# Further products that nothing reads: in both preparations, in the context's chain and in the attention's cores

## The chip, the cores and the metric

The kernel runs on one core of one Trainium2 chip. The metric is the time of one execution on the device in microseconds (us). Engines: PE is TensorE (PEld its loading of weights), DVE is VectorE, ACT is ScalarE, POOL is GpSimd, SP issues the DMAs. Each has its own queue and works it off in order; between queues the engines wait for each other by semaphores. TensorE's clock is granted at one of two levels, 1.2 or 2.4 GHz; the profile gives it as 0.50 or 1.00, or as a mean over a stretch.

## What is computed

One layer of a hybrid backbone over 256 latent tokens with a context of 256 tokens, width 1024, in float32. The parts that matter here:

```python
h_x = modulate(rms_norm(x, norm1_g[l]), m_x[0], m_x[1])
h_c = modulate(rms_norm(ctx, norm1_g[l]), m_c[0], m_c[1])
z_x = split_cols(h_x @ w_in[l]); z_c = split_cols(h_c @ w_in[l])
ya_c, ya_x = rwkv_mixer(z_c, z_x, ...)       # both directions; latent scans start from the context's state
yb_c, yb_x = na_mixer(z_c, z_x, ...)         # windowed attention with all context keys
x = x + m_x[2] * branch_merge(z_x[9], z_x[10], ya_x, yb_x, proj_a[l], proj_b[l], w_out[l])
h2_x = modulate(rms_norm(x, norm2_g[l]), m_x[3], m_x[4])
x = x + m_x[5] * moe(h2_x, router_w, router_bias, moe_w1[l], moe_w3[l], moe_w2[l])
```

The scan of the mixer is, for each of 8 heads and both directions (`...` stands for what is left out):

```python
def rwkv_scan(s0, r, decay, k, v, kk, a, reverse, emit):
    def step(s, inp):
        w_t, k_t, v_t, kk_t, a_t = inp[:5]
        s_kk = jnp.einsum('bhvk,bhk->bhv', s, kk_t)
        s = (s * w_t[:, :, None, :]
             - s_kk[..., None] * (kk_t * a_t)[:, :, None, :]
             + v_t[..., None] * k_t[:, :, None, :])
        ...
```

## The kernel before

The scan runs in chunks of 32 steps. A stream (first the context, s = 0, then the latents, s = 1) passes three parts, which the names below follow.

- The preparation, `rw_prep`, for two halves f of the heads and two directions d: `low_rank` (products of 64 rows with 256 columns, L675, and ACT's tanh, L680); `decays` (DVE L692 to L710, ACT L694 to L700, POOL L705 to L711); `products` (small products within a chunk, L727, masked by DVE L733 and copied by ACT L736; then POOL scales their left operand, L739); `turn` (transposes L749, copied out by ACT and DVE, L753). POOL and DVE share `decays`: DVE L710 needs what POOL L709 writes.
- The solve, `rw_solve`: 31 steps on DVE (L790, L792).
- The chain, `rw_chain`: 8 steps, one chunk of each direction in each, with the products x (L820), the inverse (L826), y (L838) and, for latents, z (L852).

The first preparation lies from about 80 to 133 us, the context's chain from 183 to 250, the second preparation from 264 to 348, the latent chain from 385 to 441. Behind it come the merge and, from 512 us, the experts, which stream their weights.

Beside this own work runs a filler, the generator `others`: values, projections and core of the attention for two halves g (`att_proj`, `att_core`), receptances, the modulation's rows, gates. `fill()` in the own work takes as many steps of it as the next number in the table `FILL` says; the table is the same before and after. While a filler's step is emitted, `other[0]` is true. The core (`att_core`) makes scores (L990, 64 rows by 512 columns), softmax parts on DVE and ACT (L999 to L1005), transposes (L967) and the output (L975). The dense filler products are 128x256 and 128x512 from `arena_p` and `arena_q`.

The order on each engine isn't that of the text. The framework's planner makes it when the program is built, from the dependencies, the order of the text and estimates of its own of how long each instruction takes; it is then fixed. So added instructions can change the order of others, on other engines too.

PSUM has eight banks here, four as `pa` (filler) and four as `pb` (own work); a product into a new tile waits until the bank's last reader is through.

`warm(p, site, n)` puts products into PE's queue that nothing reads: bf16, 128 rows by 128 columns of weights, n columns streamed (512 or 256), written into the tile p that the next real products overwrite. `WARM` gives their number at a site. Before, the sites are the steps 3 to 7 of the latent chain and the group norm behind it. A dependency without a semaphore keeps such a product behind the last product of the own work (L276).

Of the kernel before, what the change touches and what calls it, by code (L numbers as in the profile page):

```python
# [166 lines left out]
]  # L167
ORDER = [(("k0", 1), ("k1", 0))] * 3

WARM = {(w, 1, i): n for w, n in (("x", 4), ("y", 3), ("z", 2)) for i in range(3, 8)}  # L170
WARM.update({("gn", i): n for i, n in enumerate((4, 4, 10, 3, 5, 5))})
MIX = [7, 1]
DEEP = [3]

# [58 lines left out]
def hybrid_kernel(ctx: ExitStack, tc: tile.TileContext, a, out, dbg=None, stop=None):  # L233
# [20 lines left out]
    def pa(name="pa"):  # L254
        return ps.tile([128, 512], F32, tag="a", name=name, bufs=4)

    def pb(name="pb"):
        return ps.tile([128, 512], F32, tag="b", name=name, bufs=4)
# [10 lines left out]
    def warm(p, site, n=512):  # L269


        cb = lambda k, w: cst1[:, _COFF[k][1] - NEARLY:_COFF[k][1] - NEARLY + w // 2].bitcast(mybir.dt.bfloat16)
        before = own[0]
        for _ in range(WARM.get(site, 0)):
            i = T.matmul(p[:, 512 - n:], cb("ob", 128), cb("scanm", n), start=True, stop=True, skip_group_check=True)  # L275
            tc.add_manual_dep(i.ins, before.name, ORDERED, reason="not before")  # L276

    def split(dhi, dlo, src, eng):

# [291 lines left out]
    p, p2 = fout["lw"]  # L571
# [89 lines left out]
    def rw_prep(s, R):  # L661
# [6 lines left out]
        def low_rank(f):  # L668
            for i, (b, src, o) in enumerate(((wlb, lw, 0), (alb, la, 8))):
                p2 = [pb(), pb()]  # L670
                for q in range(2):
                    for d in range(2):
                        r_ = slice(64 * d, 64 * d + 64)
                        Q = 2 * f + q
                        mm(p2[d][:, q * 256:(q + 1) * 256], b[r_, Q * 128:(Q + 1) * 128], src[r_, t_])  # L675
# [37 lines left out]
        def products(f, d):  # L713
# [2 lines left out]

            w = 32 * nw
            pp = [pb(), pb()]
            for i in range(8):
                if i and i % 2 == 0:  # L720
                    fill()
# [20 lines left out]
        def turn(f, d):  # L742
            bk = tmps[d][3]
            for q in range(2):
                if q:
                    fill()
                p = pb()
                for i in range(4):
                    T.transpose(p[:, i * 128:(i + 1) * 128], bk[:, q * 8 + 2 * i:q * 8 + 2 * i + 2].rearrange("p c w t -> p (c w t)"), ident)  # L749
                pv = p.rearrange("p (i h k) -> p i h k", i=4, h=2)  # L750
# [202 lines left out]
    def att_core(g):  # L953
# [26 lines left out]
        for q in range(2):  # L980
# [4 lines left out]
                G.tensor_tensor(bi.ap, bi.ap, C["win"].unsqueeze(1).to_broadcast([128, 6, 64]), op=ALU.add)  # L985
            for b in range(2):
                pls = [pa(), pa()]
                for h in range(2):
                    r_ = slice(64 * h, 64 * h + 64)
                    mm(pls[h], qB[r_, q, b * 128:(b + 1) * 128], kB[r_, q, :])  # L990
# [517 lines left out]
```

## Time and profile before

| | |
|---|---|
| median of 3 runs | 744.21 us (742.38 to 745.29) |
| the profiled execution | 747.27 us, of which the span is 745.5 us |
| mean granted clock of TensorE in the span | 0.957 |
| PE busy | 689.3 us, 92% of the span |
| DVE, ACT, POOL busy | 397.8, 299.5, 102.0 us |
| products that nothing reads | 82, all from 408 us on |

The rows come from the one profiled execution; times in them count from the start of its span. A row of a timeline merges instructions that follow each other on an engine: start, time, engine, line, operation, out<-in with shapes, number, and in brackets the idle time before it with what ended it. A float32 product of small shape stands in the trace as two records, so x64 there can be 32 products of the program. A row of the stretches gives the length, then for each engine its busy time and the number of its instructions, the granted clock, and the share and rate of the DMAs.

### The profile page before, as it was taken

What the parts mean: (1) busy time and instruction counts of PE and PEld (TensorE: products, weight loads), DVE (VectorE), ACT (ScalarE), POOL (GpSimd) and SP (SyncE); (2) the same over time, 40 slices, a digit from 0 to 9 for tenths busy, and PEclk for the clock granted to TensorE, in tenths of its full rate; (3) what the DMA queues carried; (4) which work ended last, traced back from release to release, by engine and by line L of the source; (5) the groups of instructions that cost most, each with busy time, mean ns of one, the idle gap of its engine ahead of it and who ended that gap; (6) DMA issues with size and microseconds to landing.
All of it is one profiled execution on the core that took longest, in us unless ns stands there. A gap on an engine that the chain in (4) does not pass through costs nothing.

```text
span 745.5 us, 14598 instructions
## 1 busy us (share of the span) xinstructions
PE 689.3 (92%) x6059; PEld 459.8 (62%) x6059; DVE 397.8 (53%) x738; ACT 299.5 (40%) x604; POOL 102.0 (14%) x90
## 2 busy tenths in 40 slices
PE   4998798999999977889899998998999999999996
PEld 2666677886775744467898775995435535534532
DVE  2546975997846478777985555954213113113113
ACT  5436667446655446836444432533201101101110
POOL 0001444002322024351003211000000000000000
PEclk9999969999995996889999999999999999999999
DMA  9843011231311132668671139888999999999951
GB/s 366 338 161 113 4 56 37 81 111 30 108 30 51 63 135 87 214 234 311 202 225 61 52 137 332 316 317 320 412 408 412 410 409 412 406 411 413 408 218 60
DMA packets 46297, 165.34 MB, mean 222 GB/s; under 512 B 5392, under 2 KB 6800, under 8 KB 45328
## 3 DMA queue, kind: packets, MB, share of 16 engines
q1 hardware_dynamic: 46224, 164.34, 58.9%
q8 instruction: 49, 0.80, 0.4%
q14 instruction: 24, 0.20, 0.1%
HBM read 163.27 MB, written 1.05 MB: 220 GB/s over the span
## 4 chain that ended last, share of the span: by engine, by line
PE 70%; DVE 11%; ACT 9%; issue 6%; POOL 3%; DMA 1%; DVEq 0%; SPq 0%; ACTq 0%; POOLq 0%
PE pa L264 51%; PE pb L264 15%; ACT arena L753 2%; DVE arena_q L281 2%; ACT arena L736 2%; PE pb L275 1%; ACT arena_q L280 1%; POOL arena L709 1%; DVE arena L790 1%; POOL arena L707 1%; DVE arena L792 1%; DMA arena<-in_x_dram 1%; DVE arena L710 1%; POOL arena L705 1%; DVE arena L693 1%
## 5 line engine op out<-in xcount | busy, mean ns | idle before, releaser
L264 PE MATMUL pa<-arena_p,arena_q 128*128 128x256 f32 (+1 forms) x984 | 163.6, 315 | 7.8 <-DVE arena_q L281 2.6
L264 PEld LDWEIGHTS pa<-arena_p,arena_q 128*128 128x128 f32 x984 | 134.8, 190 | 29.6 <-issue 7.0
L264 PE MATMUL pa<-arena,arena_m 128*64 128x512 f32 (+1 forms) x652 | 148.8, 561 | 0.0
L264 PE MATMUL pb<-arena 128*32 128x64 f32 (+13 forms) x2248 | 115.6, 279 | 22.0 <-DVE arena L710 7.3
L264 PEld LDWEIGHTS pb<-arena 128*32 128x32 f32 (+7 forms) x2246 | 72.9, 144 | 60.0 <-issue 24.0
L264 PEld LDWEIGHTS pa<-arena,arena_m 128*64 128x64 f32 x652 | 48.8, 138 | 85.1 <-issue 80.3
L280 ACT CAST arena_q<-arena 128x1024 fp32r<-128x1024 f32 (+1 forms) x66 | 63.0, 955 | 79.7 <-PE pa L264 57.7
L281 DVE TENSOR_TENSOR arena_q<-arena,arena_q 128x1024 fp32r<-128x1024 f32 (+1 forms) x66 | 77.5, 1174 | 24.0 <-ACT arena_q L280 18.8
L264 PE MATMUL pa<-arena_q,arena_p 128*128 128x256 f32 x384 | 57.5, 300 | 0.0
L1408 DVE TENSOR_TENSOR arena_m<-arena_m,pa 128x512 f32<-128x512 f32 x8 | 5.5, 688 | 95.9 <-PE pa L264 95.9
L264 PEld LDWEIGHTS pa<-arena_q,arena_p 128*128 128x128 f32 x384 | 50.2, 198 | 5.8 <-issue 3.2
L813 POOL TENSOR_TENSOR arena<-arena 64x512 f32<-64x512 f32 x30 | 33.9, 1130 | 127.9 <-DVE arena L843 126.1
L1349 ACT ACTIVATE arena_m<-pa,arena 128x128 f32<-128x128 f32 x32 | 12.0, 455 | 76.4 <-PE pa L264 76.4
L264 PE MATMUL pa<-arena_p,arena_m 128*64 128x512 f32 x140 | 41.3, 593 | 0.0
L264 PE MATMUL pa<-arena 128*64 128x256 f32 (+5 forms) x192 | 41.1, 470 | 0.0
L280 ACT CAST arena_r<-arena_m 128x512 fp32r<-128x512 f32 x16 | 9.9, 618 | 66.6 <-DVE arena_m L1428 66.6
L1428 DVE SCALAR_TENSOR_TENSOR arena_m<-pa,arena,arena_p 128x512 f32<-128x512 f32 x16 | 12.0, 751 | 44.8 <-PE pa L264 44.8
L809 ACT COPY arena<-arena 32x256 f32<-32x256 f32 x64 | 25.8, 403 | 20.5 <-PE pb L264 18.5
L264 PEld LDWEIGHTS pa<-arena_m,arena 128*128 128x128 f32 x256 | 29.2, 192 | 6.6 <-issue 5.7
L264 PE MATMUL pa<-arena_m,arena 128*128 128x128 f32 x256 | 30.7, 279 | 0.9 <-DVE arena_m L1336 0.9
L843 DVE TENSOR_TENSOR arena<-pb,arena 64x512 f32<-64x512 f32 x30 | 20.6, 688 | 15.5 <-PE pb L264 14.9
L264 PE MATMUL pb<-arena,arena 64*64 64x64 f32 (+1 forms) x496 | 28.0, 257 | 0.5 <-ACT arena L829 0.5
(210 smaller groups left out, 845.5 us busy)
## 6 DMA issues: line engine op xcount, KB each, us to landing
arena<-in_w_dram SPq DMA_DIRECT2D x137, 512.0 KB, 10.0
arena<-in_win_dram SPq DMA_DIRECT2D x42, 512.0 KB, 3.8
arena_p<-in_w_dram SPq DMA_DIRECT2D x35, 512.0 KB, 10.2
arena<-in_modr_dram SPq DMA_DIRECT2D x32, 512.0 KB, 4.1
arena<-in_modw_dram SPq DMA_DIRECT2D x4, 2048.0 KB, 14.5
arena<-in_w_dram SPq DMA_DIRECT2D x20, 256.0 KB, 8.2
arena_m<-in_w_dram SPq DMA_DIRECT2D x10, 512.0 KB, 8.8
arena<-in_pab_dram SPq DMA_DIRECT2D x8, 512.0 KB, 3.3
```

The costliest lines, as they stand in the source:

```text
L264: i = T.matmul(out, lhsT, rhs, start=start, stop=stop, skip_group_check=True)
L275: i = T.matmul(p[:, 512 - n:], cb("ob", 128), cb("scanm", n), start=True, stop=True, skip_group_check=True)
L280: S.copy(dhi.bitcast(F32R), src)
L281: eng.tensor_tensor(dlo.bitcast(F32R), src, dhi, op=ALU.subtract)
L693: V.tensor_tensor_scan(cum[:, go], C["scanm"], sg[:, go], 0.0, op0=ALU.mult, op1=ALU.add)
L736: S.activation(NT[ro + 32 * d:ro + 32 * d + 32, :, 2 * f:2 * f + 2].rearrange("p t q c -> p (q c) t")[:, par::2], pv[o_ + 32 * d:o_ + 32 * ...
L753: (V.tensor_copy if h and c2 else S.copy)(BT[f][64 - 64 * h:128 - 64 * h, d, q, c2:8:2, :], pv[64 * c2:64 * c2 + 64, :, h, :])
L809: S.copy(Z[rv, h, :, d, :], vt[32 * c4:32 * c4 + 32, h, tt, :, :])
L813: G.tensor_tensor(sd[r_], Z[r_, h], pc[r_, :, :, i].rearrange("p d q -> p q d").unsqueeze(3) .to_broadcast([64, 4, 2, 64]), op=ALU.mult)
L843: V.tensor_tensor(Z1[r_, h], pyv[r_], sd[r_], op=ALU.add)
L1349: S.activation(dst, src, AF.Identity, scale=m4[:, kc:kc + 1], bias=m3[:, kc:kc + 1])
L1428: V.scalar_tensor_tensor(sil.ap, py[n2], gsl[pr % 2].ap, m5r[:, n2 * 512:(n2 + 1) * 512], op0=ALU.mult, op1=ALU.mult)
```

## The change

`WARM` gets sites in both preparations (low-rank, products, turn), in steps 3 to 6 of the context's chain (x and y) and in the attention's core (before each pair of scores), and `warm` is called there. Within a filler's step the dependency on the own work's last product is left out. No other line changes.

```diff
--- before.py
+++ after.py
@@ -167,8 +167,16 @@
 ]
 ORDER = [(("k0", 1), ("k1", 0))] * 3
 
+
 WARM = {(w, 1, i): n for w, n in (("x", 4), ("y", 3), ("z", 2)) for i in range(3, 8)}
 WARM.update({("gn", i): n for i, n in enumerate((4, 4, 10, 3, 5, 5))})
+for _s in range(2):
+    for _f in range(2):
+        WARM.update({("low", _s, _f, i): 2 for i in range(2)})
+        WARM.update({("prod", _s, _f, d): 5 for d in range(2)})
+        WARM.update({("turn", _s, _f, d): 1 + _s for d in range(2)})
+    WARM["att", _s] = 4
+    WARM.update({(w, 0, i): n for w, n in (("x", 3), ("y", 2)) for i in range(3, 7)})
 MIX = [7, 1]
 DEEP = [3]
 
@@ -273,7 +281,8 @@
         before = own[0]
         for _ in range(WARM.get(site, 0)):
             i = T.matmul(p[:, 512 - n:], cb("ob", 128), cb("scanm", n), start=True, stop=True, skip_group_check=True)
-            tc.add_manual_dep(i.ins, before.name, ORDERED, reason="not before")
+            if not other[0]:
+                tc.add_manual_dep(i.ins, before.name, ORDERED, reason="not before")
 
     def split(dhi, dlo, src, eng):
 
@@ -668,6 +677,7 @@
         def low_rank(f):
             for i, (b, src, o) in enumerate(((wlb, lw, 0), (alb, la, 8))):
                 p2 = [pb(), pb()]
+                warm(p2[i], ("low", s, f, i))
                 for q in range(2):
                     for d in range(2):
                         r_ = slice(64 * d, 64 * d + 64)
@@ -716,6 +726,7 @@
 
             w = 32 * nw
             pp = [pb(), pb()]
+            warm(pp[0], ("prod", s, f, d), 256)
             for i in range(8):
                 if i and i % 2 == 0:
                     fill()
@@ -745,6 +756,7 @@
                 if q:
                     fill()
                 p = pb()
+                warm(p, ("turn", s, f, d))
                 for i in range(4):
                     T.transpose(p[:, i * 128:(i + 1) * 128], bk[:, q * 8 + 2 * i:q * 8 + 2 * i + 2].rearrange("p c w t -> p (c w t)"), ident)
                 pv = p.rearrange("p (i h k) -> p i h k", i=4, h=2)
@@ -985,6 +997,7 @@
                 G.tensor_tensor(bi.ap, bi.ap, C["win"].unsqueeze(1).to_broadcast([128, 6, 64]), op=ALU.add)
             for b in range(2):
                 pls = [pa(), pa()]
+                warm(pls[0], ("att", g))
                 for h in range(2):
                     r_ = slice(64 * h, 64 * h + 64)
                     mm(pls[h], qB[r_, q, b * 128:(b + 1) * 128], kB[r_, q, :])
```

That makes, with 512 columns: 16 in the low-rank, 24 before turns (1 per tile for the context, 2 for the latents), 8 in the chain's y, 32 in the cores; with 256 columns: 40 before `products`, 12 in the chain's x. The line numbers of after are higher, by 8 at `mm` (L264 is L272), 9 to 12 in the preparation (L709 is L719, L711 L721, L739 L750, L705 L715, L707 L717), 12 in the chain (L813 is L825) and 12 or 13 in the core (L967 is L979), and L275 is L283.

PE's queue at the first preparation, before, from the low-rank's tail (L264 into `pb`, 128x256) to the small products (64x32) of the first half and direction; `pa` from `arena_q` is filler:

```order
L264 MATMUL pb<-arena 128x256 x8
L264 MATMUL pa<-arena_q,arena_p 128x256 x23
L264 MATMUL pb<-arena 128x512 x4
L264 MATMUL pa<-arena_q,arena_p 128x256 x34
L264 MATMUL pb<-arena 64x32 x32
```

The same place after, first up to the first of five added products:

```order
L272 MATMUL pb<-arena 128x256 x4
L272 MATMUL pa<-arena_q,arena_p 128x256 x16
L272 MATMUL pb<-arena 128x512 x4
L283 LDWEIGHTS arena
L283 MATMUL pb<-arena 128x256
```

and from the fifth of them on:

```order
L283 MATMUL pb<-arena 128x256
L272 MATMUL pa<-arena_q,arena_p 128x256 x28
L272 MATMUL pb<-arena 64x32 x32
L283 LDWEIGHTS arena
L283 MATMUL pb<-arena 128x512
```

16 and 28 filler products stand ahead of the small products where 23 and 34 stood; the rest moved behind them. Two pairs of added products of 512 columns stand ahead of the first row shown.

PE's queue at the end of the first core, before, with the products of the context's chain (64x64 y, 32x64 x and inverse) between those of the attention (128x2, 128x512):

```order
L264 MATMUL pa<-arena_q,arena_p 128x256 x6
L264 MATMUL pb<-arena,arena_73 64x64 x8
L264 MATMUL pa<-arena 128x2 x3
L264 MATMUL pb<-arena,arena_73 64x64 x7
L264 MATMUL pa<-arena 128x2
L264 MATMUL pa<-arena 128x512
L264 MATMUL pb<-arena 32x64 x16
L264 MATMUL pa<-arena 128x512
```

And after, from the last products of that chain (64x64) on:

```order
L272 MATMUL pb<-arena,arena_73 64x64 x15
L272 MATMUL pa<-arena 128x512 x2
L272 MATMUL pa<-arena_q,arena_p 128x256 x6
L979 MATMUL pa<-arena 128x128 x4
L272 MATMUL pa<-arena_q,arena_p 128x256 x2
L272 MATMUL pa<-arena 128x2 x4
L272 MATMUL pa<-arena 128x512 x2
L979 MATMUL pa<-arena 128x128 x4
L283 LDWEIGHTS arena
L283 MATMUL pa<-arena 128x512
```

The chain is through before the 128x2 products, which lie two chain steps further back in it before.

POOL's queue in the second preparation, before (L709 `decays`, L739 behind `products`, L813 the latent chain's first step, L705 and L707 the second half's `decays`):

```order
L711 COPY arena<-arena 128x2x8
L739 TENSOR_TENSOR arena<-arena 128x1024
L709 TENSOR_TENSOR arena<-arena 128x512
L782 MEMSET arena 128x1024
L783 MEMSET arena 128x32
L711 COPY arena<-arena 128x16
L739 TENSOR_TENSOR arena<-arena 128x1024
L709 TENSOR_TENSOR arena<-arena 128x512
L711 COPY arena<-arena 128x2x8
L813 TENSOR_TENSOR arena<-arena 64x512 x2
L705 TENSOR_TENSOR arena<-arena 64x16x32
```

And after:

```order
L721 COPY arena<-arena 128x2x8
L719 TENSOR_TENSOR arena<-arena 128x512
L750 TENSOR_TENSOR arena<-arena 128x1024
L721 COPY arena<-arena 128x16
L794 MEMSET arena 128x1024
L795 MEMSET arena 128x32
L719 TENSOR_TENSOR arena<-arena 128x512
L750 TENSOR_TENSOR arena<-arena 128x1024
L721 COPY arena<-arena 128x2x8
L825 TENSOR_TENSOR arena<-arena 64x512 x2
L719 TENSOR_TENSOR arena<-arena 128x512
L715 TENSOR_TENSOR arena<-arena 64x16x32
```

L709 (now L719) stands ahead of L739 (L750) both times, and the fourth of its kind ahead of the second half's four L705 and L707 (L715, L717), behind which it stood.

## Rows read from the trace of the kernel before

**Rows 1.** The page's head, PE's busy time, and of the part with 40 slices PE's busy tenths and its granted clock in tenths.

```profile
span 745.5 us, 14598 instructions
PE 689.3 (92%) x6059; PEld 459.8 (62%) x6059; DVE 397.8 (53%) x738; ACT 299.5 (40%) x604; POOL 102.0 (14%) x90
...
PE   4998798999999977889899998998999999999996
...
PEclk9999969999995996889999999999999999999999
```

**Rows 2.** Stretches from the first preparation to the end of the second, cut where the clock changes; the columns are named in the first row.

```profile
core 0: us, PE busy (x) PEld busy (x) DVE busy (x) ACT busy (x) POOL busy (x), PEclk, DMA share, GB/s
90.60:107.50 16.90, 16.75 (x167) 13.10 (x171) 13.31 (x16) 10.16 (x23) 8.25 (x5) 0.50 0.20 63
107.60:132.80 25.20, 21.40 (x277) 17.97 (x271) 16.43 (x28) 20.35 (x45) 10.75 (x8) 1.00 0.14 43
183.00:222.00 39.00, 38.98 (x547) 29.90 (x547) 26.59 (x41) 22.13 (x47) 11.35 (x10) 1.00 0.22 66
227.10:244.00 16.90, 16.90 (x161) 8.78 (x164) 9.59 (x21) 7.90 (x18) 5.81 (x6) 0.50 0.09 29
244.20:263.70 19.50, 19.50 (x198) 16.42 (x191) 6.97 (x12) 8.56 (x19) 0.00 (x0) 1.00 0.24 82
263.70:278.20 14.50, 10.94 (x66) 4.69 (x64) 11.82 (x21) 8.84 (x22) 5.11 (x4) 1.00 0.33 114
278.30:281.60 3.30, 3.21 (x73) 2.19 (x73) 3.30 (x5) 1.73 (x4) 0.96 (x1) 0.50 0.37 133
281.70:288.40 6.70, 5.28 (x36) 2.75 (x36) 5.55 (x7) 2.79 (x7) 6.21 (x5) 1.00 0.58 192
288.60:302.00 13.40, 9.57 (x104) 6.61 (x108) 11.65 (x24) 10.68 (x25) 3.25 (x4) 0.50 0.22 72
302.20:325.90 23.70, 19.59 (x200) 11.31 (x192) 16.31 (x29) 16.50 (x36) 12.77 (x9) 1.00 0.63 211
326.10:332.80 6.70, 6.20 (x52) 4.83 (x53) 4.66 (x6) 2.29 (x4) 1.93 (x1) 0.50 0.68 242
332.90:348.50 15.60, 15.41 (x167) 12.74 (x167) 10.81 (x17) 11.40 (x24) 1.94 (x1) 1.00 0.81 289
```

**Rows 3.** Timeline of PE in the first preparation: filler, the wait for `decays`, and the filler with which the stretch of low clock ends.

```profile
76.44 2.96 PE L264 MATMUL pa<-arena_q,arena_p 128*128 128x256 f32 x23
...
81.80 4.25 PE L264 MATMUL pa<-arena_q,arena_p 128*128 128x256 f32 x34
90.58 3.94 PE L264 MATMUL pb<-arena 64*64 64x32 f32 x72 [4.53 <-DVE arena L710]
...
104.34 2.93 PE L264 MATMUL pa<-arena_q,arena_p 128*128 128x256 f32 x12
```

**Rows 4.** Timeline of PE in the context's chain, around 225 us.

```profile
223.73 0.68 PE L264 MATMUL pb<-arena,arena 64*64 64x64 f32 x16 [0.47 <-ACT arena L829]
224.34 0.83 PE L264 MATMUL pa<-arena 128*128 128x2 f32 x6
225.10 0.68 PE L264 MATMUL pb<-arena,arena 64*64 64x64 f32 x14
225.71 1.44 PE L264 MATMUL pa<-arena 128*128 128x2 f32 x4
227.07 1.34 PE L264 MATMUL pb<-arena 128*32 128x64 f32 x32
```

**Rows 5.** Timeline of PE in the latent chain: products that nothing reads (L275) and the product behind them.

```profile
411.71 0.82 PE L275 MATMUL pb<-arena 128*128 128x512 bf16 x3
412.46 0.33 PE L264 MATMUL pb<-arena,arena 64*64 64x64 f32 x2
...
416.20 0.61 PE L275 MATMUL pb<-arena 128*128 128x256 bf16 x4
416.74 0.30 PE L264 MATMUL pb<-arena 128*32 128x64 f32 x4
```

**Rows 6.** Timeline of PE in the second preparation: three rows with a wait before them.

```profile
278.39 4.31 PE L264 MATMUL pb<-arena 64*64 64x64 f32 x76 [1.61 <-DVE arena L710]
...
292.43 7.42 PE L264 MATMUL pb<-arena 64*128 64x256 f32 x92 [4.80 <-ACT arena L680]
...
326.60 1.22 PE L264 MATMUL pa<-arena_p,arena_q 128*128 128x256 f32 x4 [2.13 <-DVE arena_q L281]
```

**Rows 7.** Timelines of POOL (first four rows) and of DVE in the second preparation.

```profile
284.19 2.38 POOL L739 TENSOR_TENSOR arena<-arena 128x1024 f32<-128x1024 f32 x1
286.53 1.44 POOL L709 TENSOR_TENSOR arena<-arena 128x512 f32<-128x512 f32 x1
...
322.22 1.65 POOL L707 TENSOR_TENSOR arena<-arena 64x512 f32<-64x512 f32 x1
323.95 1.27 POOL L709 TENSOR_TENSOR arena<-arena 128x512 f32<-128x512 f32 x1
...
288.01 0.69 DVE L710 TENSOR_TENSOR arena<-arena 128x512 f32<-128x512 f32 x1 [1.15 <-POOL arena L709]
...
325.25 0.69 DVE L710 TENSOR_TENSOR arena<-arena 128x512 f32<-128x512 f32 x1 [2.43 <-POOL arena L709]
325.86 0.69 DVE L281 TENSOR_TENSOR arena_q<-arena,arena_q 128x512 fp32r<-128x512 f32 x1
```

## The prediction

> **What bounds the kernel now.** I read the slices first. TensorE (PE) is busy 92% of the span, and in the line of its granted clock the 6th, the 13th and the 16th to 18th slices are below 9 [rows 1]. Then I cut that part into stretches by the clock [rows 2]. There are five at 0.50, which is 1.2 GHz, and the others run at 1.00, 2.4 GHz. In the first two PE is busy all the time (16.75 of 16.90 us, and 16.90 of 16.90), so work there took twice as long on the engine that bounds it: 8.4 and 8.45 us could come back. The other three lie in the second preparation and hold 3.21, 9.57 and 6.20 us of PE work, so 1.6, 4.8 and 3.1 us at most. All five hold 26.3 us. Until 263.7 us PE hardly rests but before 90.58 us and at the first preparation's end, so up to there the work on PE sets the time. In the second preparation PE is idle for 13.7 of 83.9 us (the sum over the last seven stretches of [rows 2]), and there a chain through POOL, DVE and ACT sets it. What comes after 348.5 us is moved as a whole.
>
> The timelines show how the clock fell. Before 90.58 us PE waits 4.53 us for DVE [rows 3]; then it works at half speed on small products. At 224 us it is not idle, but does only 128x2 and 64x64 products for some 3 us, and the clock is at half from 227 on [rows 4].
>
> **What a product costs.** The kernel has them already in the latent chain: three of 512 columns take from 411.71 to the next product at 412.46, 0.75 us or 0.25 each; four of 256 take from 416.20 to 416.74, 0.135 each [rows 5]. The change adds 80 of 512 (16 low-rank, 24 before turns, 32 in the attention's cores, 8 in the chain) and 52 of 256 (40 and 12): 20.0 + 7.0 = 27.0 us, if all lies on the path. That is as much as the clock can give back, so the result hangs on what is hidden and on what comes back. By stage:
>
> First preparation, 16 of 512 and 20 of 256: 4.0 + 2.7 = 6.7 us. Nine of them (the second low-rank's four, the five that follow) run where the clock is low and cost double, 1.7 more: 8.4. The ten of 256 and eight of 512 behind 107.6 us (1.35 + 2.0 = 3.35) find PE idle for 3.8 of 25.2 us there, with ACT busy for 20.35 [rows 2]; I count them as covered by ACT's copies. Without this cover they cost the 3.35. Does the clock still fall? The order now has 16 + 28 filler products before the wait where it had 23 + 34. At 0.125 us (4.25 us for 34, [rows 3]) the 13 fewer save 1.6 us, and the nine products there cost 4 x 0.25 + 5 x 0.135 = 1.7. So PE arrives at the wait when it did, the wait of 4.53 us stays, and the clock falls. What changes is the way back. Before, the clock rose only behind twelve filler products in a row (104.34, [rows 3]); now full-width products stand between the small ones from the low-rank on, and I take half of the stretch as returned, 4.2 of 8.4 (bounds 0 and 8.4; a half because the fall itself is the same). Sum: 8.4 - 3.35 - 4.2 = +0.85.
>
> Context chain with the first core, 24 of 512 and 12 of 256: 6.0 + 1.6 = 7.6 us, nothing hidden, as PE is busy for 38.98 of 39.00, 16.90 of 16.90 and 19.50 of 19.50 us [rows 2]. The piece in which the clock fell, the 128x2 products with 64x64 around them, now stands behind the chain, between fillers, transposes and wide products, with four added ones before and four after. It is still thin there for some 4 us, so I expect a shorter fall, not none: two thirds back, 5.6 of 8.45 (bounds 0 and 8.45). Sum: +2.0.
>
> The Trainium skill (Trainium Kernel Development and Optimization, section "Performance Expectations") says that matmul busy time is a bad measure, since matmuls are pipelined, and that the busy share of weight loads is better. In the chain that share is 29.90 of 39.00 [rows 2], so by this rule about a quarter of the 7.6 would find room: the sum here would be +0.2 and the whole 1.8 us better. The products of [rows 5] stand between just such chain products and take their whole time, with a little more, so I keep the full price.
>
> Second preparation, 40 of 512 and 20 of 256: 10.0 + 2.7 = 12.7 us. The 12 and 5 before the first wait (3.7) fall into 3.65 us of idle PE up to 281.6 [rows 2], as PE waits for DVE L710 then [rows 6]: hidden. Eight and five belong to the second low-rank, the core and the product step behind it (2.7); about 1.5 goes into the wait of 4.80 us before 292.43, but two and five (1.2) come behind the release, on the path. Twelve before turns and in the core (3.0) lie beside ACT's copies, 4.11 us idle in the stretch up to 325.9: hidden. The last ten of 256 and eight of 512 (3.35) stand where PE is full (15.41 of 15.60): on the path. Together 4.55; if no cover held, 12.7.
>
> Here the new order gives something too. POOL has L739 before L709 [rows 7]: 2.38 us on which DVE L710 waits, and behind L710 in DVE's queue the reduce, ACT's copies and the release of PE at 292.43. Now L709 goes first: -2.4. The same happens at 325.25, where L710 waits 2.43 us for an L709 behind POOL's four L705 and L707, the filler's L281 is queued behind it, and PE idles for 2.13 us [rows 6, 7]. The new order has L709 ahead of these four, so -2.1. Bounds: nothing, if ACT's queue then waits for DVE's reduces anyway, and 4.5. I take 4.5, as these waits are rows and not guesses. L739 comes later for it; the turn waits on that, but behind ACT's copies. Of the clock: the first stretch's wait is filled, but the products before 278 us may not do (0.8 of 1.6); the wait before 292.43 only shrinks (1.6 of 4.8); the third went with the idle time now gone (2.1 of 3.1). Sum: 4.55 - 4.5 - 4.5 = -4.45.
>
> All: 0.85 + 2.0 - 4.45 = -1.6 us. The profiled execution took 747.27 us, so 745.7 for one like it; the median of the runs is 744.21, 3.1 lower, and so I predict 742.6 there. The unknown terms reach far: everything on the path and no clock back would be +28.7, everything hidden and all back -30.8. Neither end is near a row: in the chain products do cost, and in the second preparation PE does idle.
>
> **The rivals.**
> A, slower: in the stage where PE never rests the products are only more work, and clock falls as long as before, because it falls in waits and thin pieces that no product fills. Place: 73 to 263.7 us. Price: the 9.8 us that I took as returned. -1.6 + 9.8 = +8.2, 752.4 us. It decides once less than 4.5 of the 16.85 us comes back (then over 3.7 slower). For it: the wait of 4.53 us stays. Against: in the latent chain, with products in every step, the clock needs no filler to stay up.
> B, faster: from the context chain on the clock holds. Then 8.45 instead of 5.6, and 9.5 instead of 4.5: -1.6 - 2.85 - 5.0 = -9.45, 734.8 us. For it: the stretches at 1.00 hold many thin pieces. Against: waits of 4.80 and 1.61 us in the second preparation that depend on other engines.
> C: the order gives nothing. ACT L736 and PE wait for another queue and the 4.5 us of order stay: +2.9, 747.1 us. For it: the attention's reduces now stand together before the product step on DVE.
>
> **How the numbers follow.** Forecast 0.34 (own range 739.5 to 746), A 0.22, B 0.26, C 0.18. A measurement tells about 0.5%, 3.7 us, from no change. Faster by more: B and a fifth of the forecast, 0.33. Slower by more: A and a quarter of C, 0.26. Between: 0.41. The range, 736 to 750, leaves out the far halves of A and B.
>
> **What would show it.** Right: the clock still falls near 90 us but rises before 107; PE at 1.00 through the chain but for a short stretch in the thin piece behind it; DVE's waits for POOL L709 (1.15 and 2.43 us in [rows 7]) nearly gone; the last turn of the second preparation some 4 us earlier against the end of the context chain's dense filler. Wrong: a low stretch as long as before in the chain (A), none after 183 us (B), PE released for the second low-rank no sooner (C), or products that take clearly less than 0.25 us between chain products.

## The result and the profile after

The changed kernel takes 751.54 us (median of 5 runs, 751.17 to 756.94) against 742.38 us (5 runs, 741.9 to 745.29): a ratio of 1.0105, 95% interval 1.007 to 1.0139. The forecast was 742.6 us, its range 736 to 750. Timed once more beside the experiments, it is 1.0088 (1.0056 to 1.0121), +6.5 us. So it is slower: by 9.2 us between the first medians, by 7.8 and 6.5 us by the two ratios. One run of the kernel before, which took 2892.54 us, is left out everywhere.

There are two profiles of it, one of an execution of 756.94 us (span 755.1) and one (run a1_whole below) of 746.34 us (span 744.5). The kernel is the same and so is the order on each engine. Of the 10.6 us between the two, 3.2 lie ahead of the first preparation, and 7.4 behind, most of them where the clock falls in the one and not in the other. The second is the fastest of its ten runs (their median is 750.41 us), and the profile of before, 747.27 us, lies above its median. So from the first row below to the end the first is 9.2 us longer than before and the second only 1.8, and neither is the median's +6.5 by itself.

The page's slices of the first of them, which answer to [rows 1]:

```profile
PE   4998789999999887989999998998999999999996
PEclk9999899999999897999999999999999999999999
```

The clock line has three slices below 9, where it had five. The stretches of before, then of the two profiles of after. They are cut at: the semaphore that lets ACT through to the first tanh of the first preparation (L680, after L690), the first step of the first solve, the last ACT copy of the receptances (L924, after L936), the last DVE copy of a turn (L753, after L765) and, for the fourth row, DVE's last instruction of the group norm (L1184, after L1197). The end piece, 282.9 us before and 283.0 in both profiles of after, is left out. Columns as in [rows 2].

```profile
75.70:132.50 56.80, 48.13 (x507) 39.15 (x503) 43.65 (x58) 40.46 (x86) 24.45 (x18) 0.85 0.13 38
132.50:263.90 131.40, 130.06 (x1373) 98.50 (x1374) 91.60 (x177) 67.93 (x136) 23.75 (x22) 0.94 0.22 68
263.90:348.10 84.20, 70.00 (x688) 44.72 (x687) 64.57 (x102) 54.07 (x119) 32.27 (x24) 0.86 0.54 184
348.10:462.60 114.50, 107.64 (x1534) 88.09 (x1532) 76.94 (x149) 44.86 (x87) 15.79 (x16) 1.00 0.52 176
```

```profile
76.10:133.00 56.90, 47.22 (x535) 37.95 (x535) 42.54 (x58) 40.14 (x85) 24.37 (x18) 0.94 0.13 38
133.00:269.00 136.00, 131.62 (x1405) 99.74 (x1414) 91.51 (x177) 68.75 (x137) 25.57 (x22) 0.96 0.21 65
269.00:356.70 87.70, 75.19 (x721) 44.49 (x724) 63.73 (x101) 54.59 (x118) 31.20 (x24) 0.94 0.51 172
356.70:472.10 115.40, 110.19 (x1551) 90.76 (x1555) 76.73 (x150) 44.87 (x88) 16.84 (x16) 0.99 0.53 180
```

```profile
72.90:129.80 56.90, 46.75 (x535) 37.53 (x537) 42.51 (x57) 40.20 (x85) 24.39 (x18) 0.94 0.13 38
129.80:261.30 131.50, 128.01 (x1405) 97.96 (x1414) 90.81 (x177) 68.64 (x136) 25.02 (x22) 1.00 0.22 68
261.30:347.60 86.30, 74.75 (x722) 44.11 (x725) 63.13 (x101) 55.02 (x118) 31.23 (x24) 0.96 0.53 175
```

Read the second number (the length) and the clock against each other. In the first preparation the clock goes from 0.85 to 0.94, and the length stays at 56.8 to 56.9 us. (The tanh itself starts 2.0 us behind this cut before and 1.4 to 1.5 after, at 77.67, 77.53 and 74.38 us; measured from there the stage is 0.6 us longer in both profiles.) In the second it goes from 0.86 to 0.94 and 0.96, and the stage is longer by 3.5 and 2.1 us. There PE is busy for 5.2 and 4.75 us more, and its idle time (length less busy time), 14.2 us before, is 12.5 and 11.55 us: it is still there. In the context's stretch the two profiles differ by 4.5 us: one holds 1.00 and is as long as before, with 7.6 us of products in it, the other falls (0.96).

The first preparation in the PE timeline of the first profile, answering to [rows 3]:

```profile
82.44 3.61 PE L272 MATMUL pa<-arena_q,arena_p 128*128 128x256 f32 x28
90.35 1.93 PE L272 MATMUL pb<-arena 64*64 64x32 f32 x64 [4.30 <-DVE arena L720]
```

The wait of 4.53 us is still 4.30. The waits of PE in the second preparation, answering to [rows 6]:

```profile
283.38 2.10 PE L272 MATMUL pb<-arena 64*64 64x64 f32 x48 [3.30 <-DVE arena L720]
...
296.92 2.07 PE L272 MATMUL pb<-arena 64*128 64x256 f32 x4 [3.58 <-ACT arena L690]
...
337.30 1.01 PE L272 MATMUL pb<-arena 128*32 128x256 f32 x18 [2.13 <-DMA arena<-in_modr_dram]
```

The wait for the decays (L720) is 3.30 us where it was 1.61. The one before the second low-rank is 3.58 us where it was 4.80. At 337.30 it is a product of the modulation's rows, which waits for its DMA. That wait was there before, too, 2.09 us, just ahead of the first row of [rows 6]:

```profile
276.15 0.64 PE L264 MATMUL pb<-arena 128*32 128x256 f32 x8 [2.09 <-DMA arena<-in_modr_dram]
```

What stands behind the 4.80 us of before, in the chain of waits (start, us, what), from the decays of the stage's first direction to the release of PE:

```profile
277.56 0.69 DVE arena L710
...
288.01 0.69 DVE arena L710
288.70 0.61 DVE arena L1002
289.33 0.81 ACT arena L1003 x2
290.17 0.60 ACT arena L736
...
292.43 7.42 PE pb L264 x92
```

And behind the 3.58 us after:

```profile
282.63 0.69 DVE arena L720
...
289.17 1.68 DVE arena L718
290.84 0.60 DVE arena L720
291.44 0.41 DVE arena L1012
...
293.10 1.52 ACT arena L1016 x4
...
294.64 0.60 ACT arena L747
...
296.92 2.07 PE pb L272 x4
```

POOL is no longer in it: L720 follows L718 at once, where L710 waited 1.15 us for L709 [rows 7]. From the end of the first decays' L710 to the end of the second's it took 10.45 us before, and it takes 8.1 now. But the attention's softmax behind it (L1002 and L1003 before, L1012 to L1016 after) stands ahead of the copies and tanh (L747, L690) that release PE with 3.2 us where it had 1.5. The last piece, 2.3 us, is as before. So 2.3 us are gained, 1.7 lost again, and the whole way, 14.2 us before, is 13.6; in the second profile it is 13.6 too.

### The profile page after: what moved, and what is told of

Its sections match the earlier page's. It is cut to its first block, busy times and chain, and to the rows that moved or that the text cites. A ratio compares the mean times of both kernels' runs of the same rounds, so it can differ in the third digit from the quotient of the medians.

```text
span 755.1 us, 14826 instructions
## 1 busy us (share of the span) xinstructions
PE 697.7 (92%) x6170; PEld 461.9 (61%) x6191; DVE 395.4 (52%) x738; ACT 301.1 (40%) x604; POOL 103.8 (14%) x90
## 4 chain that ended last, share of the span: by engine, by line
PE 49%; DVE 7%; ACT 3%; DMA 2%; issue 1%; POOL 0%; DVEq 0%; ACTq 0%
PE pa L272 36%; PE pb L272 9%; PE pb L283 2%; DVE arena_q L290 2%; DMA arena<-in_win_dram 1%; DMA arena<-in_modr_dram 1%; ACT arena L747 1%; DVE arena L802 1%; PE pa L1426 0%; DVE arena L804 0%; ACT arena_q L289 0%; PE pa L1374 0%; DVE arena L720 0%; DVE arena L715 0%; DVE arena L703 0%
## 5 line engine op out<-in xcount | busy, mean ns | idle before, releaser
L272 PE MATMUL pa<-arena_p,arena_q 128*128 128x256 f32 (+1 forms) x984 | 162.5, 313 | 4.8 <-DVE arena_p L384 1.8
L272 PEld LDWEIGHTS pa<-arena_p,arena_q 128*128 128x128 f32 x984 | 133.7, 188 | 25.1 <-issue 5.2
L272 PE MATMUL pa<-arena,arena_m 128*64 128x512 f32 (+1 forms) x652 | 148.8, 561 | 0.0
L272 PE MATMUL pb<-arena 128*32 128x64 f32 (+13 forms) x2248 | 110.6, 265 | 20.2 <-DVE arena L720 7.6
L272 PEld LDWEIGHTS pb<-arena 128*32 128x32 f32 (+7 forms) x2246 | 68.6, 134 | 57.0 <-issue 16.6
L272 PEld LDWEIGHTS pa<-arena,arena_m 128*64 128x64 f32 x652 | 48.8, 138 | 85.1 <-issue 80.3
L290 DVE TENSOR_TENSOR arena_q<-arena,arena_q 128x1024 fp32r<-128x1024 f32 (+1 forms) x66 | 75.9, 1151 | 28.5 <-ACT arena_q L289 23.5
L272 PE MATMUL pa<-arena_q,arena_p 128*128 128x256 f32 x384 | 56.1, 293 | 0.0
L272 PEld LDWEIGHTS pa<-arena_q,arena_p 128*128 128x128 f32 x384 | 48.4, 190 | 4.5 <-issue 1.7
L825 POOL TENSOR_TENSOR arena<-arena 64x512 f32<-64x512 f32 x30 | 34.8, 1160 | 114.0 <-DVE arena L855 112.1
L283 PE MATMUL pb<-arena 128*128 128x256 bf16 (+1 forms) x165 | 37.0, 324 | 7.7 <-ACT arena L747 4.8
L272 PE MATMUL pa<-arena_p,arena_m 128*64 128x512 f32 x140 | 41.3, 593 | 0.0
L272 PE MATMUL pa<-arena 128*64 128x256 f32 (+5 forms) x192 | 35.3, 459 | 0.0
L272 PEld LDWEIGHTS pa<-arena_m,arena 128*128 128x128 f32 x256 | 29.2, 192 | 6.6 <-issue 5.7
L272 PE MATMUL pa<-arena_m,arena 128*128 128x128 f32 x256 | 30.7, 278 | 0.9 <-DVE arena_m L1349 0.9
L283 PEld LDWEIGHTS <-arena 128*128 128x128 bf16 x214 | 17.6, 100 | 20.5 <-issue 14.6
## 6 DMA issues: line engine op xcount, KB each, us to landing
arena_p<-in_w_dram SPq DMA_DIRECT2D x35, 512.0 KB, 10.2
```

What stands on the lines that cost most here:

```text
L272: i = T.matmul(out, lhsT, rhs, start=start, stop=stop, skip_group_check=True)
L290: eng.tensor_tensor(dlo.bitcast(F32R), src, dhi, op=ALU.subtract)
L825: G.tensor_tensor(sd[r_], Z[r_, h], pc[r_, :, :, i].rearrange("p d q -> p q d").unsqueeze(3) .to_broadcast([64, 4, 2, 64]), op=ALU.mult)
```

## The experiments

Two theories to begin with. Theory 1, added work: each part costs its products' time where PE has no rest, less the clock that it brings back in its own stage. Theory 2, new order: the loss is what the planner's new order does on the queues. Line numbers of the runs are those of after, or 2 to 6 higher. Where a ratio is turned into us, it is by the median of before that was timed beside the run (744.3 to 745.1 us). The times and ratios are of 6 to 12 runs; a stage's length is of the one profiled execution.

**The four parts alone.** Each keeps one part of the table's additions and leaves out the others. The first preparation:

```diff
+WARM.update({("low", 0, f, i): 2 for f in range(2) for i in range(2)})
+WARM.update({("prod", 0, f, d): 5 for f in range(2) for d in range(2)})
+WARM.update({("turn", 0, f, d): 1 for f in range(2) for d in range(2)})
```

> Only the first preparation's sites (16 products of 512 columns, 20 of 256, 6.7 us of TensorE time); the other four parts of the table as before. Theory 1 (added work): what the change costs is the products' time where TensorE has no rest, less the clock that they bring back in their own stage; then this part shows the +0.5 us that the stage up to the first solve showed in the whole change, and nothing behind it: 0 to +1 us in the total. Theory 2 (new order): the loss is the planner's new order behind the sites (attention behind the context's chain, waits moved in the second preparation, filler of the gates late); then this part alone, whose order differs from before far into the second preparation, already costs 3 to 5 us, and the time stands behind 133 us.

Measured: 1.0038 (1.0011 to 1.0066), +2.8 us, more than theory 1 and just less than theory 2 had. The profiled execution, 744.67 us, is one of its shorter ones. In it the first preparation takes 57.0 us, as before. In the two rows behind it no product was added, but the planner's order is another one. The second preparation takes 87.4 us instead of 84.2, with 15.9 us of idle time, which speaks for theory 2. The context's stretch takes 124.6 us instead of 131.4, for the clock holds at 1.00 in it:

```profile
131.10:255.70 124.60, 123.63 (x1372) 95.41 (x1376) 92.41 (x177) 68.84 (x137) 23.04 (x22) 1.00 0.22 67
255.70:343.10 87.40, 71.52 (x690) 44.19 (x687) 62.29 (x99) 54.51 (x119) 30.37 (x24) 0.88 0.56 187
```

The context's chain:

```diff
+WARM.update({(w, 0, i): n for w, n in (("x", 3), ("y", 2)) for i in range(3, 7)})
```

> Only the context chain's sites (8 products of 512 columns, 12 of 256, 3.6 us). The planner's order changes little here: POOL and SP stand as before, and only the chain's tail is arranged anew. Theory 1: +3.6 us less the part of the 8.45 us of the low stretch at 227 us that comes back, about +1 (0 to +2). Theory 2: as little order changes, about the same with the opposite cause: within +-1 us of before. This run prices the products with hardly any change of order, so it bounds theory 1: over +3 would mean that no clock comes back here.

Measured: 0.9959 (0.9939 to 0.9979), -3.1 us: faster than both kernels, and below what either theory expected. The stage, to be laid beside the second row of before above:

```profile
131.90:257.40 125.50, 123.94 (x1389) 96.72 (x1394) 91.03 (x177) 68.42 (x137) 23.75 (x22) 1.00 0.23 71
```

It is 5.9 us shorter, with 3.6 us of products more in it, and the clock holds at 1.00 throughout. If the products cost their full price, 9.5 us came back, for the 8.45 of [rows 2]. But the chain's tail also stands in another order here, and in p1_firstprep an order alone, without a product in this stretch, held the clock as well and made it 6.8 us shorter. So the gain is the change of table and order together; what of it is the products' no run separates.

The attention's cores:

```diff
+WARM.update({("att", 0): 4, ("att", 1): 4})
```

> Only the attention cores' sites (32 products of 512 columns, 8.0 us: 16 in the context chain's stage, 16 in the second preparation). Theory 1: the first 16 cost their 4.0 us less returned clock, the second 16 lie half in idle time: +3 to +5 us. Theory 2: +4 to +6, of which most stands in the second preparation, where the order of POOL and DVE changes, as waits and not as TensorE's busy time.

Measured: 1.0038 (1.0011 to 1.0065), +2.8 us, just below what both expected. The median clock of its runs is 0.968 against 0.961. So of the 8.0 us of products 5.2 are hidden or paid back by the clock; in which shares isn't shown.

The second preparation:

```diff
+WARM.update({("low", 1, f, i): 2 for f in range(2) for i in range(2)})
+WARM.update({("prod", 1, f, d): 5 for f in range(2) for d in range(2)})
+WARM.update({("turn", 1, f, d): 2 for f in range(2) for d in range(2)})
```

> Only the second preparation's sites (24 products of 512 columns, 20 of 256, 8.7 us); up to 264 us the kernel stands as before. Theory 1: 8.7 us less what lies in the stage's 14 us of idle time and less the returned clock: -2 to +1 us. Theory 2: the one POOL step that moves here (L719 ahead of four L715 and L717) moves the wait and does not remove it, idle time of the stage stays at 12 to 14 us, and the part costs +2 to +4 us.

Measured: 1.0031 (1.0006 to 1.0056), +2.3 us, with 8.7 us of products. The size is theory 2's, the place isn't: the stage takes 85.0 us in the profile, and its idle time falls from 14.2 to 9.8 us, where theory 2 had 12 to 14. So of 8.7 us of products 4.4 went into idle time here.

**The whole, and the order by itself.** The parts add up to +4.9 us (unrounded). Three more runs take order and products apart. `PLACES` holds the order of one kernel on its five queues, without the added products, and imposes it on the other by dependencies without a semaphore:

```diff
+    for e, packed in PLACES.items():
+        own_q = [x for x in traced if str(x.engine) == "EngineType." + e]
+        order = list(itertools.accumulate(json.loads(zlib.decompress(base64.b85decode(packed)))))
+        for a_, b_ in zip(order, order[1:]):
+            tc.add_manual_dep(own_q[b_], own_q[a_].name, ORDERED, reason="place")
```

Where the products are to cost next to nothing, `warm` cuts those of the added sites to 8 columns:

```diff
+        if site[0] in ("low", "prod", "turn", "att") or site[1] == 0 and site[0] in ("x", "y"):
+            n = 8
```

First the whole change, unedited:

> The whole change, beside the runs below on one chip, as their measure: +5 to +10 us against before. The four parts alone made +2.8, -3.0, +2.8 and +2.3 us, together +4.9. Theory 1 (added work, part by part): the whole is the sum, +5 us, within what the intervals leave open. Theory 2 (new order): the parts' orders make each other worse, and the whole lies clearly above the sum, +8 or more.

Measured: 1.0088 (1.0056 to 1.0121), +6.5 us, between the two theories. With the sum of the parts at +4.9, what only the whole has is +1.6 us, with an uncertainty of some 4.5 us.

The order of after, 8 columns:

> The order of the changed kernel on all five queues, imposed by dependencies without a semaphore, but the 132 added products stream 8 columns each, where they had 512 or 256. What is left of them is the loading of their weights. Theory 1 (added work): without their columns there is next to nothing to pay and next to no clock is brought back, so the time is that of before, -1 to +2 us. Theory 2 (new order): the waits that the order makes are all there and the clock isn't brought back, so the loss is as large as in the whole change or larger, +6 to +12 us.

Measured: 1.011 (1.0066 to 1.0154), +8.2 us, which seemed to be theory 2's.

The order of before, all columns:

> All 132 added products with their full columns, but every other instruction stands on its queue in the order of the kernel before. Theory 1 (added work): the order gives and takes nothing, so the time is that of the whole change, +5 to +9 us. Theory 2 (new order): the loss was the order's, the products and the clock they bring back are about even, -3 to +3 us.

Measured: 1.0201 (1.0164 to 1.0239), +15.0 us. Neither theory has this: with the products in, the old order is worse than the new one by 8.4 us.

The order of before, 8 columns:

> The fourth corner to the two runs with an imposed order: the order of the kernel before, and the 132 added products with 8 columns each. It prices what is left of such a product (its weights' load and its place in the queue), so that the order's own share can be read from the run with the new order and 8 columns, which made +8.2 us. In that run's trace five such products in a row take 0.13 to 0.21 us, 0.03 to 0.04 each, so 132 of them 4 to 5 us if all lie on the path. If the order is the cost: +1 to +3 us here, so 5 to 7 us are the order's. If the small rest of the products is the cost: +6 to +9 us here, and the order's share is next to nothing.

Measured: 1.0109 (1.007 to 1.0147), +8.1 us: the second case. Against +8.2 in the new order the order's own share is +0.1 us, with an uncertainty of some 4 us on it. So with 8 columns the 5 to 7 us that theory 2 gave to the order are not in the total, and the forecast's -4.5 us lies at the edge of that. Imposing an order isn't by itself what costs: c1_waits and o5_bank below, with an imposed order, are no slower than p2_chain, whose order it is. So the +8.1 us is put down to the 132 nearly empty products: by estimate 2.6 us for the clock, which is lower (median 0.952 against 0.958; the rate is worked out below), and 5.5 us, 0.042 each, for themselves.

With all columns, the new order makes +6.5 where the old one makes +15.0; why the products cost less in it isn't shown. The second preparation of the three runs (old order with products, new order and old order with 8 columns):

```profile
267.30:358.90 91.60, 75.84 (x742) 44.62 (x745) 67.20 (x102) 54.34 (x119) 31.38 (x24) 0.96 0.51 173
```

```profile
259.60:350.60 91.00, 76.09 (x730) 46.99 (x729) 63.88 (x102) 54.73 (x118) 30.62 (x24) 0.83 0.49 167
```

```profile
267.80:351.90 84.10, 71.97 (x745) 45.44 (x744) 65.06 (x102) 54.09 (x119) 32.39 (x24) 0.88 0.55 185
```

In the first, the clock holds (0.96) and PE's idle time is 15.76 us, more than before: in sum the products fill none of it. Between the second and the third the order differs, and with it the places of the products. In this stage that is not nothing: the new order takes 6.9 us more, with 2.8 us more idle time and a lower clock. What cancels it in the total lies elsewhere; in the context's stretch the new order holds the clock at 1.00 even with 8 columns, and takes 129.6 us where the old one takes 132.2 at 0.94:

```profile
130.00:259.60 129.60, 124.59 (x1413) 96.83 (x1414) 90.74 (x177) 68.59 (x137) 25.43 (x22) 1.00 0.22 68
```

**The one move that the forecast counted as a gain.** No product; every queue in the old order, but POOL from the second preparation on in the new one:

```diff
-L754 TENSOR_TENSOR arena<-arena 128x1024
 L723 TENSOR_TENSOR arena<-arena 128x512
+L754 TENSOR_TENSOR arena<-arena 128x1024
... (the same once more, and what lies between)
+L723 TENSOR_TENSOR arena<-arena 128x512
 L719 TENSOR_TENSOR arena<-arena 64x16x32
 L721 TENSOR_TENSOR arena<-arena 64x16x32
 L719 TENSOR_TENSOR arena<-arena 64x16x32
 L721 TENSOR_TENSOR arena<-arena 64x16x32
-L723 TENSOR_TENSOR arena<-arena 128x512
```

> No added product, every queue in the order of the kernel before, but POOL's in the second preparation in that of the changed kernel: L719 of the forecast's text stands ahead of L750 three times, and the last time ahead of four L715 and L717 as well. The forecast's step: DVE no longer waits for POOL there, and 4.5 us go: -3 to -5 us. Its rival: ACT's and PE's queues then wait for the next thing: -1 to +1 us. A third: L750 now comes late and holds up the turns behind it: +1 to +4 us.

Measured: 1.0061 (1.0028 to 1.0095), +4.5 us: the third case, and with the opposite sign to the forecast. The second preparation takes 88.2 us there, with 16.7 us of idle time. PE's waits:

```profile
290.02 7.42 PE L274 MATMUL pb<-arena 64*128 64x256 f32 x92 [2.35 <-ACT arena L694]
...
306.44 1.97 PE L765 MATMUL pb<-arena 128*128 128x128 f32 x8 [3.35 <-POOL arena L754]
```

and POOL's queue ahead of the second of them:

```profile
303.05 1.45 POOL L723 TENSOR_TENSOR arena<-arena 128x512 f32<-128x512 f32 x1 [6.66 <-ACT arena L714]
304.45 1.93 POOL L754 TENSOR_TENSOR arena<-arena 128x1024 f32<-128x1024 f32 x1
```

Before, this step of POOL was:

```profile
298.98 1.93 POOL L739 TENSOR_TENSOR arena<-arena 128x1024 f32<-128x1024 f32 x1 [1.30 <-PE pb L264]
```

The wait of 4.80 us shrinks to 2.35, as forecast. But the scaling of the left operand (L754, L739 before) now queues behind an L723 that itself waits for ACT. It starts 14.4 us behind the release of PE, where it started 6.6 us behind it, and the turn's transposes wait 3.35 us for it. In the whole change the other queues move with POOL, and this wait isn't in it; but of the gain 0.6 us is left there.

**Products only where PE waits.** The order of p2_chain, imposed, with its sites and two more:

```diff
+WARM.update({("prod", 0, 0, 0): 28, ("prod", 1, 0, 0): 16})
```

> The order of the kernel with the context chain's sites alone, imposed, and products at three places only: the chain's sites, 28 of 256 columns (3.8 us) before the first small products of the first preparation, where TensorE waits 4.52 us for DVE L720, and 16 (2.2 us) before those of the second preparation, where it waits 2.90 us. Theory 1: products that lie in a wait for data cost nothing there; if the wait shrinks to 0.7 us and the clock no longer falls behind it, up to 8.4 us of the first preparation's low stretch come back on top of the -3.0 of the chain: -5 to -11 us against before. If it stays at -3, either the products delay what TensorE waits for, or the clock falls all the same.

Measured: 0.9949 (0.9919 to 0.998), -3.8 us: short of the -5 to -11 of theory 1, and no more than the chain's sites alone within the interval. The PE timeline of the first preparation of p2_chain, then of this run:

```profile
89.82 3.94 PE L272 MATMUL pb<-arena 64*64 64x32 f32 x72 [4.52 <-DVE arena L720]
...
98.20 3.08 PE L272 MATMUL pb<-arena 64*128 64x256 f32 x36 [1.85 <-ACT arena L690]
```

```profile
87.46 2.20 PE L274 MATMUL pb<-arena 64*64 64x32 f32 x72 [1.14 <-DVE arena L724]
...
95.95 3.08 PE L274 MATMUL pb<-arena 64*128 64x256 f32 x36 [3.69 <-ACT arena L694]
```

The wait is filled (4.52 to 1.14) and the clock stays up for the 72 small products (3.94 to 2.20 us). And then the next wait is longer, by 1.84 us, about what the clock had given. Both runs need 8.4 to 8.5 us from the start of the first row to that of the second. The other engines' chain sets the time between these two rows. The 16 products ahead of the second preparation's first small products shorten the wait there too (2.90 to 1.82 us), but the next one stays at 4.80 us, and that stage takes 85.4 us where p2_chain takes 83.8.

The same base, with one other site, ahead of the second half's second low-rank:

```diff
+WARM.update({("low", 1, 1, 1): 12})
```

> The order of the kernel with the context chain's sites alone (-3.0 us), imposed, with its sites, and 12 products of 512 columns (3.0 us) ahead of the second half's second low-rank, where TensorE waits 4.80 us for ACT L690. If products fill the wait for an engine: they cost nothing and shorten the low stretch behind it, -3 to -6 us against before. If they themselves wait, because the tile that they write is the one whose bank ACT has to give back: they come behind the wait, at half clock 6 us long at most, and the run is 3 to 5 us slower than its base: 0 to +2 us against before. The trace tells directly whether the wait of 4.80 us stands before the products or is gone.

Measured: 0.9948 (0.9917 to 0.9979), -3.9 us. Each theory has a half of it:

```profile
283.23 4.44 PE L285 MATMUL pb<-arena 128*128 128x512 bf16 x12 [3.75 <-ACT arena L694]
287.60 4.45 PE L274 MATMUL pb<-arena 64*128 64x256 f32 x92
...
297.11 0.66 PE L765 MATMUL pb<-arena 128*128 128x128 f32 x4 [2.35 <-ACT arena L751]
```

The wait stands before the products: they write the tile whose bank ACT has to give back, so they can't fill it. They add 4.4 us behind it. But the 92 products that follow run in 4.45 us where they took 7.42, and the next wait is 2.35 us where it was 0.74 (both from the trace of p2_chain). The stage takes 85.8 us against 83.8 there; in the total the products cost nothing and gain nothing measurable.

**What a low clock costs.** The 77 runs of before that were compared with these experiments differ in where the clock fell. The 21 with a mean clock of 0.965 or more have a median span of 741.3 us (clock 0.966), the 22 of 0.957 or less one of 745.85 (0.9555). A mean that is higher by 0.0105 over 743 us is 15.6 us less at half clock, and it goes with 4.55 us: an estimate of 0.29 us for each.

The first preparation gives the same. In six profiles (before, p2_chain, p3_att, p4_secondprep, o4_poolorder, o5_bank) it has no added product and the same products in the same order. Its length goes with its clock: 55.9 us twice at 0.88, 56.8 and 56.9 at 0.85, 58.1 and 58.2 at 0.82. From 0.82 to 0.88 that is 7.5 us less at half clock and 2.3 us: 0.31 for each. Here are p4_secondprep and o4_poolorder, and o2_oldorder_products, with the change's products in the old order and the clock at 0.86:

```profile
74.40:130.30 55.90, 45.83 (x507) 37.55 (x503) 43.68 (x57) 40.39 (x85) 24.48 (x18) 0.88 0.13 39
```

```profile
73.20:131.40 58.20, 49.46 (x507) 40.35 (x503) 43.73 (x58) 40.84 (x85) 24.43 (x18) 0.82 0.12 37
```

```profile
74.80:135.60 60.80, 51.69 (x539) 41.18 (x539) 43.87 (x58) 39.99 (x85) 23.71 (x18) 0.86 0.12 36
```

The Trainium skill (TensorE: Matmul & The Clock Gate, "Terms") puts the penalty at the throttled time times one less the ratio, 0.5 here. The chain's stage, where PE never rests, comes near it: 16.9 us at half clock are gone, and 6.8 us come back in p1_firstprep, 5.9 in p2_chain with its products in the stretch. The first preparation and the kernel as a whole stay below it; c1_waits shows one place why: there the slow products run into a wait that is there anyway.

## Why the prediction was wrong

- **First preparation, +0.85.** Measured +0.1 by the rows, +0.6 from the tanh itself, in both profiles: right, and both sides of the sum came near. Of 17.0 us at half clock 6.8 are left; 10.2 us at 0.31 are 3.2 us back, by estimate, where 4.2 were counted. The products, 8.4 less 3.35, cost 4.0 us in the old order at nearly the same clock (60.8 against 56.8; 4.5 from the tanh). But the premise that low clock costs a half here, because PE "bounds" the stage, was too high: it is about a third. The wait that stays held.
- **Context chain with the first core, +2.0.** Measured +4.6 and +0.1 in the two profiles, depending on whether the clock falls in the attention's tail. That the clock can hold here is confirmed by p1_firstprep and p2_chain. The price of a product is not: p2_chain shows only what is left of price and return together, so it doesn't decide between the full price and three quarters of it, which the prediction weighed. The reason that it gave, the new place of the thin piece, is borne out: in p1_firstprep and o1_neworder_noproducts another order holds the clock without the products' columns.
- **Second preparation, -4.45: the step that failed.** Measured +3.5 and +2.1, 8.0 and 6.6 us off, where the whole median missed by 8.9. In the forecast's terms PE was to be busy for 8.2 us more (12.7 of products less 4.5 of clock) and idle for 12.65 less (8.15 filled by products, 4.5 taken away by the order). It is busy for 5.2 and 4.75 more, so more clock came back than was counted, and idle for only 1.7 and 2.65 less. So the idle time that was counted as filled or removed is what failed, by 10 to 11 us. The runs show three pieces of it:
  - *The order's -4.5.* DVE's waits for L709 did go from 1.15 and 2.43 us to 0 and 1.11. But of the 2.4 us counted for the first of them, 2.3 arrive at L720 and 1.7 are lost to the longer softmax behind it, so 0.6 us is left. POOL's move alone costs 4.5 us (o4_poolorder), and all queues together, with nearly empty products, cost 6.9 us in this stage and 0 in the total.
  - *The 3.65 us up to 281.6 us, "as PE waits for DVE L710 then".* Only 1.61 us of it was that wait; 2.09 was the wait for the DMA of the modulation's rows, which is 2.13 us at another place after. The wait for the decays is 3.30 us after.
  - *The 1.5 us into the wait before the second low-rank.* Products that write the tile that is waited for wait themselves (o5_bank).

  How much each is of the 10 to 11 us stays open.
- **What comes after, "moved as a whole".** Nearly: +0.9 us up to the end of the group norm in the first profile, -0.6 in the second (114.50 to 115.40 and 113.90).
- **The rivals.** A's time (752.4) came closest, but not its reason: the clock did come back. What was said against A, that the clock needs no filler in the latent chain, no row shows: filler (`pa` from `arena_p` and `arena_q`) stands between its steps before, too. C's reason, the attention's reduces that now stand together, is in the chain above; its 747.1 was 4.4 us short. By the 0.29 us above, the clock's 0.019 (0.961 to 0.980, the medians of before and of a1_whole) is 28 us less at half, and 8.2 us; the forecast had 14.3. With 6.1 us less for the clock and 4.5 less for the order, its sum of -1.6 comes to +9.0, and +6.5 to +9.2 was measured. That is an estimate that fits the total, not a proof of its terms: by stages the idle time of the second preparation is the difference.
- **What wasn't tried.** Which of the second preparation's waits cost how much in the whole change; the new order without any added product, imposed on the kernel before; and the chain's sites in the old order.

## What to carry to other kernels

A clock that falls costs less than the half that it takes from TensorE, as far as other engines set the time: here some 0.4 us for each us at half clock in the chain, where TensorE never rests, 0.31 in the first preparation and 0.29 over the kernel. So before counting a low stretch as gain, look at the next wait behind it: if one follows within a few microseconds, its slack can take the gain, as in c1_waits. One idle microsecond can be spent once: on hidden work, on a wait that an order removes, or on a faster clock; and before spending it, read what it waits for. And where a planner makes the order, an added product changes two things, so a part of a change that pays (here one part of the table, -3.1 us, was worth more than all four) isn't yet the products' gain.

## What the runs showed that was not expected

- Nearly empty products aren't free: 132 with 8 columns made the kernel 8.1 us slower (o3_oldorder_noproducts), about as much as the full ones in the planner's order (+6.5, within the intervals).
- In the context's chain the clock held at 1.00 without any added product, by another order of the same products (p1_firstprep, one profile).
- One kernel, one order, two executions: 744.5 and 755.1 us of span, at a mean clock of 0.984 and 0.976. A single profile of such a kernel is worth its run's time only beside its clock.
- With no added product ahead of it, the first tanh of the first preparation starts between 74.6 (c1_waits) and 78.4 us (p3_att); stages are better measured from there than from zero.
